# An ordered section that begins one gate group earlier, in a conv, latent-attention and memory block

## The chip, the cores and the metric

The kernel runs on one core of one Trainium2 chip. The metric is the time of one execution in device microseconds; lower is better. "Before" is the kernel as it stood, "after" is the same kernel with the diff below. Engines are named as in the profile: PE (matmuls), PEld (its weight loads), DVE, ACT, POOL and SP. SP issues the loads of weights, ACT issues most stores, POOL issues most other loads.

## The reference

512 tokens of width 2048 in float32, one layer. One input projection feeds three branches and their gates; the gated branches go through one output projection and are added to the input.

```python
h = rms_norm(x, norm_g)
(c_gate, b_gate, u, conv_z, c_q, c_kv, k_rope_raw, mla_z,
 mem_q, mem_z, g_conv, g_mla, g_mem) = split(h @ w_in)
conv_y = b_gate * causal_depthwise_conv(c_gate * u, conv_w)            # width 1024
o_conv = (conv_y * silu(conv_z)) @ w_conv_out
mla_y  = mla_attention(c_q, c_kv, k_rope_raw, cos, sin, ...)           # 16 heads
o_mla  = (mla_y * silu(mla_z)) @ w_mla_out
mem_y  = memory_attention(mem_q, mem, mem_norm_g, w_mem_kv, ...)       # 4 heads of 256
o_mem  = (mem_y * silu(mem_z)) @ w_mem_out
merged = sigmoid(g_conv) * o_conv + sigmoid(g_mla) * o_mla + sigmoid(g_mem) * o_mem
return x + merged @ w_o
```

The part around the change is the memory attention: 256 memory tokens of width 2048 are normalised and multiplied by `w_mem_kv` into keys and values; each of the four heads normalises its queries and keys, takes a softmax over the 256 tokens and multiplies by the values. The rotary tables `cos` and `sin`, which the latent attention needs later, are made in the same stretch.

## The kernel before, in words

**Products.** Every float32 operand is split into two float32r parts, a high part (`whi` for weights, rounded by ACT) and a low part (`wlo`, the rest, subtracted by DVE), and a product is three matmuls, high by high, high by low, low by high. The large projections use a two-by-two scheme with seven products, P1 to P7, in place of eight; some of them first need sums or differences of two weight blocks on DVE (`raw<-raw`). The forms of weights rotate through six buffers, which is three pairs.

**Steps.** The work is a list of steps. Each step makes the forms of one piece of weights and has 12 matmuls of 512 columns (in the stages looked at here). The forms of a step are issued one step ahead of its products. Hooks hang other work behind a step: `after(i, f)` calls `f` once step `i` is issued. `here` holds the step being issued. A gate group (`gate_group`) is 28 steps; its results are evicted from PSUM, go through a sigmoid and are stored to DRAM (`gdram<-r`). `last_s` is the first step of the last gate group, `first_m` the first step of the memory stage, 28 steps later.

**The last gate group and mem.** In the gate group hang `mem_load(j)`, four loads of the transposed memory tokens issued by POOL into `mraw`; `mem_cut(j)`, which splits each load into high and low parts `mT` (ACT and DVE, with the norm's gain) and squares it; and `mem_sum`, which adds the squares and turns them into the norm's factors with 16 matmuls of one column. The `mT` tiles lie in the buffers (tag `blk`) that hold the activations used by products P1 and P5 of the gate group.

**The memory stage.** Four weight groups of eight steps (keys, values, keys, values) with the heads hung between them. A head (`mem_attend`) is a generator in five parts, called step by step: it loads its queries (`rows<-mqdram`, two buffers, POOL), normalises, transposes and splits them (`q`), multiplies by the keys, takes the softmax (`p`), turns it (`ph`), and multiplies by the values. `rotary_tables` is hung at step 3 of the stage: loads of `pos_i`, `invf`, `rgain` and `mask` on POOL, then a chain of small operations on DVE that begins with the copy of `pos_i` to `pos_f`. `open_two`, at the stage's beginning, closes the pool `work` (tag `q` and others, which hold the gate groups' results) and opens the pools `lat`, `kv`, `memq` and `latrow` where it lay.

**Order.** Three ways stand side by side. SP's loads keep the order in which they are written. Ordinary code is put in order by the language's own scheduler. A noted section is put in order by the kernel itself: `nc.start()` begins to note every call as an `Op` (engine, estimated cost, tiles, what it depends on), and `nc.play()` runs a list scheduler over them (`order`) and issues them in that order on each engine. In it every engine is free at time zero, and an operation whose inputs were made before the section is ready at time zero. A tile that is written for the first time in the section takes a buffer of its tag; buffers of tiles that are only read in it count as taken until their last noted use; tiles that are not touched in it are not known. Among operations that could start at the same earliest time the one of lowest rank goes first. A matmul's rank is its place in the program. Other operations take the rank of the first matmul that depends on them, or their own place plus `away`:

```python
op.prio = min([op.idx + away + op.away] + [s.idx if s.eng == "PE" else s.prio for s in op.succs])
```

There are two noted sections. The first covers the beginning of the kernel. The second begins with the memory stage's third step (`TURN = 2`) and reaches to the end of the latent attention. Calls issued by a noted section bear line 250 in the profile, all other calls line 246. `nc.fence()` is called in the second section when the pools of the memory stage are closed: what first writes a tile of the pools `mla` and `proj` must then wait, in the order, for every noted operation on `latrow`, `memq` and `kv`. In the issued program every operation waits for what it really depends on, whatever the order.

Of the kernel before, what the change touches and what calls it, by code (L numbers as in the profile page):

```python
# [43 lines left out]

WARM = 5
RELAX = 600
START = 32
TURN = 2
LINE = 512
SMALL_FILL = 64  # L50
TOP_FILL = 120
# [48 lines left out]
class Player:  # L100
# [6 lines left out]
            setattr(self, n, Queue(self, getattr(nc, n), self.QUEUES[n]))  # L107

    def start(self):
        self.ops, self.access, self.first, self.fenced, self.lastpe = [], {}, {}, None, {}  # L110

    def fence(self):

        self.fenced = [o for o in self.ops
                       if any(p in str(self.first[t][1]) for t in o.tiles for p in ("_latrow_", "_memq_", "_kv_"))]

    def add(self, eng, call, kind, writes, reads):
        op = Op()
        op.eng, op.call, op.idx, op.kind, op.away = eng, call, len(self.ops), kind, self.away
        op.occ, op.lat = cost(eng, kind, writes, reads)  # L120
        op.preds, op.succs, op.gets, op.tiles = set(), [], [], []
        for ap, store in [(a, False) for a in reads] + [(a, True) for a in writes]:
            t = ap.tensor
            dims = list(ap.ap)
            on_chip = ap.space != bass.MemoryType.DRAM
            lo = ap.offset % dims[0][0] if on_chip else ap.offset
            hi = lo + sum(s * (n - 1) for s, n in dims[on_chip:]) + 1
            for o, l, h, st in self.access.setdefault(t.name, []):
                if (store or st) and l < hi and lo < h and o is not op:
                    op.preds.add(o)  # L130
            self.access[t.name].append((op, lo, hi, store))
            if on_chip:
                if t.name not in self.first:
                    self.first[t.name] = (op, str(t.cap_key), t.tag_meta.bufs)
                    op.gets.append(t.name)
                    if any(p in str(t.cap_key) for p in ("_mla_", "_proj_")):
                        op.preds.update(self.fenced)
                elif self.first[t.name][0] is not op:
                    op.preds.add(self.first[t.name][0])
                if t.name not in op.tiles:  # L140
                    op.tiles.append(t.name)
                if store and eng == "PE":
                    if t.name in self.lastpe:
                        op.preds.add(self.lastpe[t.name])
                    self.lastpe[t.name] = op
        for o in op.preds:
            o.succs.append(op)
        self.ops.append(op)
# [108 lines left out]
def cost(eng, kind, writes, reads):  # L257

    n = max(int(np.prod(a.shape[1:])) for a in (writes[:1] if kind != "tensor_reduce" else reads))
    if kind == "dma_start":  # L260
        return {"SP": (max(0.45, n * LOAD), 4.5), "ACT": (0.37, 4.5), "POOL": (0.7, 5.0)}[eng]
    if eng == "PE":
        occ = 0.109 if kind == "transpose" else max(n, 136) / 2250
        return occ, occ + 0.25
    if eng == "ACT":
        occ = 0.0009 * n + (0.045 if reads[0].space != bass.MemoryType.PSUM else 0.02)
        occ += 0.09 * (len(reads) > 1) + 0.1 * (len(writes) > 1)
    elif eng == "DVE":
        occ = n / 960 + 0.067 + 0.06 * (kind == "scalar_tensor_tensor")
    else:  # L270
        occ = 0.33 + 0.165 * n
    return occ * ROOM, occ * ROOM + 0.2


def body(ctx, tc, a, out):
    nc = Player(tc.nc)
# [4 lines left out]
    def open_pool(name, side="left", bufs=1):  # L281
        es = ExitStack()
        p = es.enter_context(tc.tile_pool(name=name, bufs=bufs, side=side, reuse_waits="tile"))
        return Lines(p, small, name), es.close
# [14 lines left out]
    def split(src, hi, lo, g=None):  # L299
        act.activation(hi, src, AF.Copy, scale=1.0 if g is None else g)  # L300
        if g is None:
            vec.tensor_tensor(out=lo, in0=src, in1=r32(hi), op=ALU.subtract)
        else:
            vec.scalar_tensor_tensor(out=lo, in0=src, scalar=g, in1=r32(hi),
                                     op0=ALU.mult, op1=ALU.subtract)

    def mm3(o, s, m, start, stop, shared=False):


        nc.tensor.matmul(o, lhsT=s[0], rhs=m[0], start=start, stop=False, skip_group_check=shared)  # L310
        nc.tensor.matmul(o, lhsT=s[0], rhs=m[1], start=False, stop=False, skip_group_check=shared)
        nc.tensor.matmul(o, lhsT=s[1], rhs=m[0], start=False, stop=stop, skip_group_check=shared)
# [31 lines left out]
    def g(col):  # L344
        return gains[:, col:col + 1]
# [30 lines left out]
    def q(name, dtype=F32):  # L376
        return work.tile([P, 2, 512], dtype, tag="q", name=name, bufs=NQ)
# [4 lines left out]
    def blk(name="blk", dtype=F32R):  # L382
        return ph.tile([P, 2, 512], dtype, tag="blk", name=name, bufs=8)
# [9 lines left out]
    def flat(t):  # L393
        return t.rearrange("p k n -> p (k n)")
# [49 lines left out]
    here = [0]  # L444

    def run_range(i0, i1):
        ws = steps[i0].forms()
        for i in range(i0, i1):
            here[0] = i
            for p in steps[i].parts:  # L450
                p(ws)
                yield
            if i + 1 < i1:
                ws = steps[i + 1].forms()
            for f in steps[i].after:
                f()

    def run_all(gen):
        for _ in gen:
            pass  # L460
# [145 lines left out]
    def after(i, f, front=False):  # L606
        steps[i].after.insert(0 if front else len(steps[i].after), f)
# [224 lines left out]
    def t_results(put, direct, early=None, add=None, own=True):  # L832
# [4 lines left out]
        def results(name, bk):  # L837
# [9 lines left out]
            if name == "P5":  # L847
                for tt in range(2):
                    vec.tensor_tensor(out=v[:, tt], in0=bk["Z"][tt], in1=v[:, tt], op=ALU.add)
                if add:  # L850
                    vec.tensor_tensor(out=flat(v), in0=flat(v), in1=flat(add(1, 1)), op=ALU.add)
                if early:
                    early(0, 1)
# [8 lines left out]
            if name in ("P4", "P6") and seen >= {"P4", "P6"}:  # L862
                r = q("r")
                for tt in range(2):
                    vec.tensor_tensor(out=r[:, tt], in0=bk["Y"][tt], in1=u[:, tt], op=ALU.add)
                if add:
                    vec.tensor_tensor(out=flat(r), in0=flat(r), in1=flat(add(0, 1)), op=ALU.add)
                    vec.tensor_tensor(out=flat(u), in0=flat(u), in1=flat(add(1, 0)), op=ALU.add)
                put(0, 1, r)
                if early:  # L870
                    early(0, 0)
# [88 lines left out]
    last_s = len(steps)  # L960
# [5 lines left out]
    def mem_load(j):  # L966
        mraw[j] = q("mraw")
        nc.gpsimd.dma_start(flat(mraw[j]).rearrange("p (k m) -> p k m", k=4), a["memT"][:, 4 * j:4 * j + 4])

    def mem_cut(j):  # L970
        m = flat(mraw[j]).rearrange("p (k m) -> p k m", k=4)
        for c in range(2):
            t = blk("mT")
            for k in range(2):
                n = 4 * j + 2 * c + k
                cols = slice(k * M, (k + 1) * M)
                split(m[:, 2 * c + k], t[:, 0, cols], t[:, 1, cols], g(G_MEM + n))
                mT[n] = (t[:, 0, cols], t[:, 1, cols])
        act.activation(flat(mraw[j]), flat(mraw[j]), AF.Square)
# [13 lines left out]
        vec.tensor_scalar(out=me, in0=v, scalar1=EPS, scalar2=None, op0=ALU.mult)  # L993

    for j in range(4):
        after(last_s + 15 + j, lambda j=j: mem_load(j))
        after(last_s + 20 + j, lambda j=j: mem_cut(j))

    P2 = {}

    def open_two():
        close_work()
        for name in ("lat", "kv", "memq", "latrow"):
            P2[name], P2["close_" + name] = open_pool(name, "left")

    first_m = len(steps)
# [39 lines left out]
    for grp in (0, 2, 1, 3):  # L1046
        d_group(a["w_mem_kv"][grp], mT, "acc", mem_results(grp), "T", nb=2)
    end_m = len(steps)
    after(first_m - 1, mem_sum)
    after(first_m - 1, open_two)  # L1050


# [69 lines left out]
    lat = {}  # L1122

    def rotary_tables():
        nc.away = RELAX
        rotary_work()
        nc.away = 0

    def rotary_work():
        pc, pcr = P2["lat"], P2["latrow"]  # L1130
# [127 lines left out]
    for s, f in ((3, rotary_tables), (20, latent_loads), (22, key_scales), (23, key_rotary), (26, query_scale)):  # L1258
        after(first_m + s, f)
# [3 lines left out]
    early_steps = run_range(0, end_m)  # L1263
    for i in range(first + 16 + START):
        next(early_steps)
        if i == first + 15:
            mark = len(nc.ops)
    nc.play(tc, (), len(nc.ops) - mark, 100)
    while here[0] < first_m + TURN:
        next(early_steps)  # L1270
    nc.start()
    run_all(early_steps)

    cqT, ckT = [None] * 4, [None] * 4
# [28 lines left out]
    key_blocks()  # L1303
    for name in ("latrow", "memq", "kv"):
        P2["close_" + name]()
    nc.fence()
    pa, close_a = open_pool("mla", "left")
    pp, close_p = open_pool("proj", "left")
    cosq, sinq = lat["tabs"]["q"]
# [436 lines left out]
```

## Time and profile before

| | |
|---|---|
| three runs, median (lowest to highest) | 2101.43 us (2100.23 to 2102.2) |
| profiled execution, its own time | 2101.0 us |
| its span, first to last instruction | 2099.1 us |
| mean granted clock of PE | 0.998 |
| busy: PE, PEld, DVE, ACT, POOL | 99%, 85%, 78%, 50%, 7% of the span |
| last gate group on PE | about 1119 to 1200 us |
| memory stage's weight products on PE | 1200 to 1321 us |

Busy time is the time in which an engine has an instruction under way. In a row of the order of time stand start, length, engine, line, operation, output and inputs, and in brackets the idle time of the engine before it and what it waited for. In the windows view each row is one stretch: its length, then for each engine busy time and instructions, the granted clock, the share of the DMA engines and GB/s.

### The profile page before, as it was taken

The numbers are of one execution on the slowest core, as the hardware profiler recorded it, in microseconds if no ns is written. First come the engines' busy times: TensorE is split into PE (matmuls) and PEld (weight loads), VectorE is DVE, ScalarE is ACT, GpSimd is POOL, SyncE is SP. The second block draws the span as 40 slices with busy tenths as digits, with TensorE's granted clock in tenths as the row PEclk, the third lists the DMA queues.
The fourth block names the chain that finished last, engine by engine and source line by source line (L and its number), as shares of the span: only waits on it lengthen the run. The fifth ranks groups of instructions, "written<-read, shape, count | busy, mean of one in ns | idle before, by whom it ended". The sixth has DMA issues, their size and how long they took to land.

```text
span 2099.1 us, 28548 instructions
## 1 busy us (share of the span) xinstructions
PE 2080.2 (99%) x10818; PEld 1792.6 (85%) x10818; DVE 1640.9 (78%) x2162; ACT 1059.5 (50%) x1524; POOL 148.4 (7%) x183
## 2 busy tenths in 40 slices
PE   9999999999999999999999989999999999999999
PEld 9888888887899988899888878888988888888887
DVE  6887788788777787777787777888887688867987
ACT  6544344344444445444445556577776344433543
POOL 0000000000000000000000011123221201110000
PEclk9999999999999999999999999999999999999999
DMA  7346444444534445534546554422332767675672
GB/s 262 124 161 201 134 137 143 144 135 133 189 121 124 148 131 184 177 121 149 167 144 225 201 187 156 146 71 78 109 106 96 289 227 203 207 230 176 202 241 75
DMA packets 106331, 338.66 MB, mean 161 GB/s; under 512 B 11088, under 2 KB 11616, under 8 KB 106192
## 3 DMA queue, kind: packets, MB, share of 16 engines
q1 hardware_dynamic: 71360, 251.92, 36.9%
q0 software_dynamic: 13792, 45.57, 7.2%
q10 hardware_dynamic: 21040, 39.33, 5.0%
q8 instruction: 85, 1.39, 0.3%
q14 instruction: 54, 0.44, 0.1%
HBM read 292.61 MB, written 44.17 MB: 160 GB/s over the span
## 4 chain that ended last, share of the span: by engine, by line
PE 95%; DVE 2%; issue 1%; DMA 1%; ACT 1%; POOL 0%; ACTq 0%; DVEq 0%; POOLq 0%
PE aux L246 38%; PE acc L246 30%; PE aux L250 14%; PE acc L250 14%; DMA raw<-in_w_ckv 0%; DVE wlo L246 0%; DVE cv L246 0%; DVE raw L246 0%; ACT whi L246 0%; DVE wlo L250 0%; DMA raw<-in_w_mlaz 0%; DMA pos_i<-in_pos 0%; DVE ang L250 0%; DVE r L246 0%; DVE s L246 0%
## 5 line engine op out<-in xcount | busy, mean ns | idle before, releaser
L246 ACT ACTIVATE whi<-raw 128x1024 fp32r<-128x1024 f32 x491 | 519.2, 1060 | 745.5 <-PE aux L246 342.6
L246 DVE TENSOR_TENSOR wlo<-raw,whi 128x1024 fp32r<-128x1024 f32 x491 | 596.8, 1221 | 276.9 <-ACT whi L246 274.1
L246 DVE TENSOR_TENSOR raw<-raw 128x1024 f32<-128x1024 f32 x258 | 315.0, 1222 | 9.2 <-DMA raw<-in_w_mla_out 1.9
L246 PE MATMUL aux<-whi,b 128*128 128x512 f32 x896 | 293.2, 389 | 1.4 <-ACT whi L246 1.4
L246 PE MATMUL aux<-whi,f 128*128 128x512 f32 x880 | 289.7, 390 | 0.0
L246 PE MATMUL acc<-whi,b 128*128 128x512 f32 x880 | 287.2, 390 | 0.8 <-ACT whi L246 0.7
L246 PEld LDWEIGHTS aux<-whi,b 128*128 128x128 f32 x896 | 168.0, 188 | 37.0 <-ACT whi L246 2.2
L246 PEld LDWEIGHTS acc<-whi,b 128*128 128x128 f32 x880 | 164.8, 188 | 35.6 <-ACT whi L246 1.9
L246 PEld LDWEIGHTS aux<-whi,f 128*128 128x128 f32 x880 | 165.0, 188 | 34.3 <-ACT E L246 0.3
L246 PE MATMUL aux<-wlo,b 128*128 128x512 f32 x448 | 174.4, 389 | 0.0
L246 PE MATMUL aux<-wlo,f 128*128 128x512 f32 x440 | 172.1, 391 | 1.0 <-DVE wlo L246 0.9
L246 PE MATMUL acc<-wlo,b 128*128 128x512 f32 x440 | 171.7, 390 | 0.0
L250 DVE TENSOR_TENSOR wlo<-raw,whi 128x1024 fp32r<-128x1024 f32 (+3 forms) x122 | 135.4, 1116 | 38.9 <-ACT whi L250 30.5
L250 ACT ACTIVATE whi<-raw 128x1024 fp32r<-128x1024 f32 (+3 forms) x122 | 118.1, 975 | 93.1 <-PE acc L250 48.6
L246 PE MATMUL acc<-whi,f 128*128 128x512 f32 x448 | 140.5, 389 | 0.0
L246 PEld LDWEIGHTS aux<-wlo,f 128*128 128x128 f32 x440 | 82.6, 188 | 20.1 <-DVE wlo L246 3.0
L246 PEld LDWEIGHTS aux<-wlo,b 128*128 128x128 f32 x448 | 84.1, 188 | 17.7 <-DVE wlo L246 0.2
L246 PEld LDWEIGHTS acc<-whi,f 128*128 128x128 f32 x448 | 84.1, 188 | 17.5
L246 PEld LDWEIGHTS acc<-wlo,b 128*128 128x128 f32 x440 | 82.6, 188 | 17.0
L246 PE MATMUL acc<-wlo,f 128*128 128x512 f32 x224 | 87.2, 389 | 0.0
L250 POOL TENSOR_TENSOR rs_r<-rs_t,mhalf 128x2 f32<-128x2 f32 (+1 forms) x71 | 69.9, 987 | 217.8 <-DVE rs_t L250 182.0
L246 POOL DMA_DIRECT2D mraw<-in_memT x4 | 2.3, 582 | 1082.7 <-DMA gdram<-r 1070.2
(392 smaller groups left out, 4096.9 us busy)
## 6 DMA issues: line engine op xcount, KB each, us to landing
raw<-in_w_conv SPq DMA_DIRECT2D x80, 512.0 KB, 4.0
raw<-in_w_gmem SPq DMA_DIRECT2D x44, 512.0 KB, 4.0
raw<-in_w_mla_out SPq DMA_DIRECT2D x44, 512.0 KB, 4.9
raw<-in_w_o SPq DMA_DIRECT2D x44, 512.0 KB, 4.4
raw<-in_w_gconv SPq DMA_DIRECT2D x40, 512.0 KB, 4.3
raw<-in_w_gmla SPq DMA_DIRECT2D x40, 512.0 KB, 3.8
raw<-in_w_mlaz SPq DMA_DIRECT2D x32, 512.0 KB, 4.2
raw<-in_w_mem_kv SPq DMA_DIRECT2D x32, 512.0 KB, 3.9
```

Of the source, the lines that this page charges most:

```text
L246: return f(*args, **kw)
L250: self.player.add(self.eng, lambda: f(*args, **kw), kind, writes, reads)
```

## The change

`TURN` goes from 2 to -24: the second noted section begins 24 steps before the memory stage, behind the products of step 4 of the last gate group. What is noted there up to the memory stage's first step gets `AWAY = 300` added to its place (`AWAYTO = 0`), so that work on which no matmul depends ranks later. The loads of mem hang at steps 8 to 11 of the gate group instead of 15 to 18, the cuts at steps 12, 15, 18 and 21 instead of 20 to 23, the sum at step 24 instead of 27. `fence` now takes the pools that it is about and keeps a list; a second call in `open_two` lets whatever first writes a tile of `lat`, `kv`, `memq` or `latrow` wait, in the order, for every noted operation on `work`. `rotary_tables` puts back the value of `away` that it found.

```diff
+AWAY, AWAYTO = 300, 0
 START = 32
-TURN = 2
+TURN = -24
...
-        self.ops, self.access, self.first, self.fenced, self.lastpe = [], {}, {}, None, {}
-
-    def fence(self):
-
-        self.fenced = [o for o in self.ops
-                       if any(p in str(self.first[t][1]) for t in o.tiles for p in ("_latrow_", "_memq_", "_kv_"))]
+        self.ops, self.access, self.first, self.fences, self.lastpe = [], {}, {}, [], {}
+
+    def fence(self, closed, opened):
+
+        if self.ops is not None:
+            self.fences.append(([o for o in self.ops if any(p in str(self.first[t][1]) for t in o.tiles
+                                                            for p in closed)], opened))
...
-                    if any(p in str(t.cap_key) for p in ("_mla_", "_proj_")):
-                        op.preds.update(self.fenced)
+                    for old, opened in self.fences:
+                        if any(p in str(t.cap_key) for p in opened):
+                            op.preds.update(old)
...
     for j in range(4):
-        after(last_s + 15 + j, lambda j=j: mem_load(j))
-        after(last_s + 20 + j, lambda j=j: mem_cut(j))
+        after(last_s + 8 + j, lambda j=j: mem_load(j))
+        after(last_s + 12 + 3 * j, lambda j=j: mem_cut(j))
...
     def open_two():
         close_work()
+        nc.fence(("_work_",), ("_lat_", "_kv_", "_memq_", "_latrow_"))
...
-    after(first_m - 1, mem_sum)
+    after(last_s + 24, mem_sum)
     after(first_m - 1, open_two)
...
     def rotary_tables():
-        nc.away = RELAX
+        usual, nc.away = nc.away, RELAX
         rotary_work()
-        nc.away = 0
+        nc.away = usual
...
     while here[0] < first_m + TURN:
         next(early_steps)
     nc.start()
+    nc.away = AWAY
+    while here[0] < first_m + AWAYTO:
+        next(early_steps)
+    nc.away = 0
     run_all(early_steps)
...
-    nc.fence()
+    nc.fence(("_latrow_", "_memq_", "_kv_"), ("_mla_", "_proj_"))
```

## The prediction

> **What bounds the kernel.** I read the page first, for the engine shares and the slices of the span, then the list of PE's waits, the chain that ended last where the longest wait is, and the order of time of the engines there.
>
> ```profile
> span 2099.1 us, 28548 instructions
> PE 2080.2 (99%) x10818; PEld 1792.6 (85%) x10818; DVE 1640.9 (78%) x2162; ACT 1059.5 (50%) x1524; POOL 148.4 (7%) x183
> PE   9999999999999999999999989999999999999999
> ```
>
> PE works nearly without a break, so a change of order alone can win only PE's idle time, 2099.1 - 2080.2 = 18.9 us, and what the clock loses around it. One slice is below nine tenths, at about 1210 to 1260 us: the beginning of the memory stage. By stages, in the windows view (PE, PEld, DVE, ACT and POOL busy, then granted clock and DMA):
>
> ```profile
> 1119.00:1200.00 81.00, 80.53 (x363) 66.51 (x363) 69.62 (x76) 48.02 (x60) 3.29 (x5) 1.00 0.57 185
> 1200.00:1262.00 62.00, 54.83 (x276) 45.56 (x275) 41.66 (x82) 36.33 (x81) 10.13 (x14) 0.94 0.59 196
> 1262.00:1640.00 378.00, 377.46 (x2116) 335.51 (x2115) 299.96 (x794) 258.11 (x603) 92.06 (x107) 1.00 0.34 111
> ```
>
> The last gate group runs in the first row, the memory stage in the second and in the beginning of the third, attention after it. The noted section now begins about 1207. Its later part leaves 0.54 us idle in 378; the stretch at its front leaves 7.17 in 62. The waits of PE between 1207 and 1262 (in all, times, longest):
>
> ```profile
> PE acc L250 <- DVE wlo L250: 6.3, 1, 6.3
> PE aux L250 <- DVE p L250: 0.7, 1, 0.7
> PE aux L250 <- DVE kn L250: 0.2, 1, 0.2
> ```
>
> One wait makes nearly all of it. The chain that ended last goes through it like this:
>
> ```profile
> 1219.89 0.70 ACT q L246
> 1220.59 0.23 issue
> 1220.82 0.80 POOL rows L250
> 1221.62 0.55 POOL kraw L250
> 1222.17 3.03 DMA pos_i<-in_pos
> 1225.20 0.02 issue
> 1225.22 0.17 DVE pos_f L250
> ```
>
> A weight's low part (wlo) stands in DVE's queue behind pos_f, the first operation of the rotary tables; pos_f waits for a small load; that load stands in POOL's queue behind a load of rows, and that one waited 8.58 us for head 0:
>
> ```profile
> 1188.22 0.80 POOL L246 DMA_DIRECT2D rows<-mqdram  x1
> 1189.83 0.76 POOL L250 DMA_DIRECT2D rows<-mqdram  x1 [0.81 <-DMA gdram<-r]
> 1220.82 0.80 POOL L250 DMA_DIRECT2D rows<-mqdram  x1 [8.58 <-ACT q L246]
> 1207.39 0.17 DVE L250 MEMSET zero<- 128x128 f32 x1 [4.70 <-DMA gdram<-r]
> 1220.61 1.41 DVE L246 SCALAR_TENSOR_TENSOR q<-aux,gains,q 128x512 fp32r<-128x512 f32 x2 [5.88 <-ACT q L246]
> 1225.22 0.17 DVE L250 CAST pos_f<-pos_i 128x4 f32<-128x4 int32 x1 [3.20 <-DMA pos_i<-in_pos]
> ```
>
> L246 marks what was issued outside the noted section, L250 what was noted and put in order. All three long DVE waits (4.70, 5.88 and 3.20, together 13.8 us) come of the seam between the two. Head 0's load and its q are L246. The order does not know that head 0 holds one of the two rows buffers, so it took the third load (head 2's) for free and set it ahead of the rotary loads. It does not know either that the new pools lie where stores of the gate group are still read, so it set the memset of zero first.
>
> **What that seam costs**, from PE's own order of time:
>
> ```profile
> 1217.66 0.39 PE L250 MATMUL acc<-wlo,mT 128*128 128x512 f32 x1
> ...
> 1218.34 0.39 PE L250 MATMUL acc<-wlo,mT 128*128 128x512 f32 x1
> ...
> 1220.05 0.71 PE L250 MATMUL acc<-whi,mT 128*128 128x512 f32 x2
> 1227.03 0.80 PE L250 MATMUL acc<-wlo,mT 128*128 128x512 f32 x1 [6.28 <-DVE wlo L250]
> ...
> 1230.16 0.62 PE L250 MATMUL acc<-whi,mT 128*128 128x512 f32 x2
> ```
>
> Three matmuls start in 0.68 us, so 0.227 each. The two of 1220.05 are due to end at 1220.50, the next starts at 1227.03: 6.53 us lost. Seven start between 1227.03 and 1230.16 (3.13 us where 1.59 is the pace): the clock comes back late, 1.54 us more. Together 8.07 us. On that second term the Trainium skill bears, "TensorE: Matmul & The Clock Gate", Part 1: after an idle window of about 3.4 us PE runs at half clock until it has been busy for about as long, and the length varies from run to run. An estimate from that page is 3.4 x 0.5 = 1.7 us, which would make the sum 8.2; the trace's 1.54 agrees, and the measured value stays in the sum. By the same page a wait much shorter than the window costs only itself.
>
> **The change, part by part.**
>
> *Beginning the noting 24 steps before the memory stage (TURN).* Nothing is added on the chip; no instruction, byte or semaphore's work is different in count. Head 0's load, its squares, its transposes and q, and all four rows tiles come inside the section. The order then knows that the third rows load needs head 0's transposes, and the rotary loads no longer have to stand behind it. This takes away the chain above: -8.07 us. What is late next is found below under the rivals. The seam itself moves to step 4 of the gate group. The first memory product stands at 1200.4:
>
> ```profile
> L246 PE MATMUL acc<-whi,mT x20: 389/389/389, 1200.4 to 1207.0; 128*128 128x512 f32 x20
> ```
>
> A step is 12 matmuls, 2.72 us at the pace above; 24 steps before 1200.4 is 1135 for PE, and the forms are made a step or two ahead of it, so the seam lies near 1131. What can stand wrongly at a seam is what the order takes for ready at its own time zero: loads into buffers still in use, and first writes of new pools. There it finds only the four loads of mem (POOL, nothing else in its queue) and weight forms that come in their natural order. I price the new seam at 0; its cover is the lead of the forms over PE (six form buffers, three steps). Its bounds: below, nothing; above, the old seam again, 8.07.
>
> *Loading, splitting and summing mem at earlier steps.* The words speak of smaller pieces; the diff leaves the bodies of the three functions alone. It is the same four loads, sixteen splits, four squares and three adds, hung at other steps, the splits three steps apart instead of one.
>
> ```profile
> 1107.23 0.73 POOL L246 DMA_DIRECT2D mraw<-in_memT  x1 [1061.14 <-DMA gdram<-r]
> ...
> 1130.59 0.53 POOL L246 DMA_DIRECT2D mraw<-in_memT  x1 [9.05 <-DMA gdram<-r]
> L246 ACT ACTIVATE mT<-mraw,gains x16: 492/493/496, 1147.0 to 1164.5; 128x256 fp32r<-128x256 f32 x16
> L246 DVE SCALAR_TENSOR_TENSOR mT<-mraw,gains,mT x16: 476/478/479, 1148.4 to 1167.4; 128x256 fp32r<-128x256 f32 x16
> L246 DVE TENSOR_TENSOR mraw<-mraw x3: 1216/1218/1224, 1156.6 to 1172.3; 128x1024 f32<-128x1024 f32 x3
> DMA to landing us min/median/max: 3.9/5.3/6.2
> ```
>
> The loads already issue by 1130.59 and land by about 1136, and between their old and new steps no other buffer of that tag is taken, so they keep their buffers and times. The splits write where the gate group's P1 and P5 operands lie; they begin at 1147.0 because product P5 has to be done with them, and no hook can make that sooner. DVE's part is 16 x 0.478 + 3 x 1.22 = 11.3 us, and it had 81.00 - 69.62 = 11.4 us idle in the gate group's stretch. Price 0, under that idle time. With the cover gone, where they stand ahead of forms, up to 11.3 us; below, the one small wait of PE there:
>
> ```profile
> PE aux L246 <- ACT whi L246: 0.5, 1, 0.5
> ```
>
> *The lower rank for the gate group's other work (AWAY).* Evictions, sigmoids and stores of the group rank 300 places later. They only fill gaps, but they free accumulators that the memory stage takes. Forms outrank them, and the forms run out of buffers after three steps, so gaps come. Price 0, covered by DVE's 11.4 us idle; uncovered, the last group's eviction adds of about 0.7 us each stand before the first memory product, a few us.
>
> *The fence.* First writes of the lat, kv, memq and latrow pools are put after every noted operation on the work pool, the last store of the group included. That ends the 4.70 us wait of zero at DVE's head. It also forbids the early rows loads of 1188.22 and 1189.83: they come after the store is down, 1207.4. That is 19 us later on POOL's queue, with the rotary loads behind them. PE has dense products of the memory stage to run meanwhile, eight steps of 2.72 for the first weight group, up to about 1222. Price 0 under those; bounds in the first rival. The kept value of away around the tables changes nothing, since it is 0 there.
>
> **The sum.** The profiled execution took 2101.0 us, 1.9 more than its span, and the runs shown have a median of 2101.43, so it stands 0.4 below. From 2101.0: -8.07 for the seam. The small waits of the stretch, 0.5 + 0.7 + 0.2 = 1.4 us, partly go and partly come anew because everything up to the end of the attention is laid out again; the row of 0.54 us idle in 378 says that such an order leaves little. I put them at 2.0 instead of 1.4, +0.6. That gives 2093.5 us. If they all go, 2101.0 - 8.07 - 1.4 = 2091.5; with another microsecond or two of new ones, 2095.
>
> **The rivals.**
>
> *The wait comes back behind the fence.* Head 0's squares began at 1207.01, just as the fence opens:
>
> ```profile
> 1201.95 0.37 ACTq L246 DMA_DIRECT2D gdram<-r  x1
> 1207.01 0.40 ACT L246 ACTIVATE sq<-rows 128x256 f32<-128x256 f32 x1
> DMA to landing us min/median/max: 3.8/6.8/9.2
> ```
>
> A rows load issued at 1207.4 lands 6.8 us later, 1214.2, so head 0's chain is 7.2 us later than now. If q then stands at the head of ACT's and DVE's queues as it does now, the forms behind it are late by up to 7.2, and 1.54 of clock follows: 8.7 against the 8.07 won, 2101.6, the same. For it: q did block DVE for 5.88 us. Against: this time the order knows when the load lands and can set forms ahead; nothing needs head 0's q before its scores, which also need the first weight group's keys, evicted and turned after 1222. Half of it would be 2097.
>
> *Slower: the splits of mem stand too early in the order.* Each of the four cuts waits for a P5 product to let go of its operands. If the order sets a cut two steps of 2.72 us (12 matmuls of 0.227) too early, ACT and DVE hold all forms behind it for 5.4 us, four times: 21.8 us, 2101.0 - 8.07 + 21.8 = 2114.7. It decides from 12.3 us, 3.1 us per cut; one step each (10.9 us, 2103.8) is still within what can be told apart. For it: DVE is full where these splits run:
>
> ```profile
> 1160.00:1180.00 20.00, 19.53 (x86) 15.80 (x86) 20.00 (x26) 10.53 (x14) 0.00 (x0) 1.00 0.27 87
> ```
>
> Against: the order's own cost of such a matmul, 512/2250 = 0.2276 us, is within 0.5% of the 0.227 measured, so it knows the release of each operand to well under a step, and the three steps between the cuts leave room.
>
> *The stall is hidden anyway.* It would have to be made up later for the change to be worth nothing. PE is busy 377.46 of the next 378 us, so nothing makes it up; I leave it no chance of its own.
>
> **How the numbers follow.** About 0.2% (4.2 us) is what a measurement of this kernel can tell from no change. The seam's wait goes and only small ones come: 0.65, 2091 to 2097, taken at 2093.5. The wait comes back in part or whole: 0.22, 2096 to 2103, of which a third is still faster by over 0.2%. The splits or the late evictions stand in the way: 0.13, 2100 to 2115 and more, mostly slower. That makes faster 0.72, same 0.17, slower 0.11. From 2091 to 2102 some 0.86 is held; the likeliest case's own range is 2091 to 2097.
>
> **What would show it.** In the changed profile: L250 operations from about 1131; no PE wait over 2 us from 1119 to 1262; granted clock 1.00 in that stretch; the slice of eight tenths back at nine; the third rows load after the rotary loads on POOL; zero no longer waiting for a gate store; head 0's rows load after 1200. Wrong if PE waits for wlo behind q or mT, or for an accumulator at the first memory product.

## The result, and the profile after

| | before | after |
|---|---|---|
| median of the runs timed side by side (lowest to highest) | 2101.81 us (2100.23 to 2103.39) | 2090.58 us (2090.26 to 2091.75) |
| ratio, 95% interval | | 0.9947 [0.9934, 0.996] |
| profiled execution, its span | 2101.0 us, 2099.1 us | 2090.99 us, 2089.2 us |

The kernel became faster by 11.2 us by medians and by 10.0 us from profiled execution to profiled execution. Forecast were 2093.5 us and a range of 2091.0 to 2102.0: the direction is right, the gain was larger than forecast, and the time lies 0.4 us below the range. In the changed kernel noted calls bear line 253 and all others line 249. Its page, first the span and the busy times, then the slices:

```profile
span 2089.2 us, 28542 instructions
PE 2077.5 (99%) x10818; PEld 1792.6 (86%) x10818; DVE 1642.0 (79%) x2162; ACT 1060.1 (51%) x1525; POOL 149.8 (7%) x183
PE   9999999999999999999999999999999999999999
```

The slice of eight tenths is gone. The two stretches of the gate group and of the stage's beginning in the windows view (length, then PE, PEld, DVE, ACT and POOL busy, granted clock, DMA share, GB/s):

```profile
1119.00:1200.00 81.00, 81.00 (x366) 67.06 (x365) 69.45 (x78) 46.59 (x59) 0.00 (x0) 1.00 0.50 157
1200.00:1262.00 62.00, 61.95 (x317) 52.08 (x316) 47.86 (x90) 41.97 (x92) 15.69 (x20) 1.00 0.69 238
```

In the second row PE is busy 61.95 us instead of 54.83 and does 317 matmuls instead of 276; the granted clock is 1.00 instead of 0.94. From 1119 to 1640 us the list of PE's waits has one line left:

```profile
PE acc L253 <- DVE qt L253: 0.5, 1, 0.5
```

The engines around the old seam, in order of time (start, length, engine, line, operation, tiles, idle before and what ended it):

```profile
1129.81 3.50 DVE L253 TENSOR_TENSOR raw<-raw 128x1024 f32<-128x1024 f32 x3
...
1200.89 1.55 POOL L253 DMA_DIRECT2D rows<-mqdram  x2
...
1204.39 0.54 POOL L253 DMA_DIRECT2D pos_i<-in_pos  x1
...
1222.56 0.80 POOL L253 DMA_DIRECT2D rows<-mqdram  x1 [4.69 <-DVE rs_t L253]
...
1210.31 0.17 DVE L253 MEMSET zero<- 128x128 f32 x1
...
1221.13 0.16 DVE L253 CAST pos_f<-pos_i 128x4 f32<-128x4 int32 x1
...
1223.10 1.40 DVE L253 SCALAR_TENSOR_TENSOR q<-aux,gains,q 128x512 fp32r<-128x512 f32 x2
```

The third rows load now stands behind the rotary loads, `pos_i` is asked for at 1204.39 instead of 1222.17, and `zero`, `pos_f` and `q` have no idle time in brackets: each stands in DVE's queue at a place where its input is there. The 1129.81 row is the first noted one on DVE; noted loads of mem issue on POOL from 1053.46 on.

**Where the 10 us came from.** Two groups of PE bracket the noted section's reach in both kernels: the products `aux<-b,whi`, all done well before the last gate group, and the part of `acc<-whi,acth` that is not noted, which begins after the noted section. A row gives their count, least, median and longest length in ns, and first and last start. Before, then after:

```profile
L246 PE MATMUL aux<-b,whi x384: 283/283/283, 614.6 to 968.9; 128*128 128x256 f32 x192
L246 PE MATMUL acc<-whi,acth x96: 389/389/477, 1651.2 to 1915.5; 128*128 128x512 f32 x96
```

```profile
L249 PE MATMUL aux<-b,whi x384: 282/283/284, 614.7 to 969.0; 128*128 128x256 f32 x192
L249 PE MATMUL acc<-whi,acth x96: 388/389/477, 1640.8 to 1905.9; 128*128 128x512 f32 x96
```

From the last start of the one to the first start of the other there are 682.3 us before and 671.8 after, 10.5 less; 0.1 was lost ahead of that stretch and 0.5 behind it. This length, called the stretch below, is compared in the experiments too, as it leaves out what happens elsewhere; run 1 has none, since its profiled execution was a slow one (2958.88 us at a granted clock of 0.656). Where in the stretch, PE's order of time tells, taken from start to start. Before:

```profile
1170.26 0.84 PE L246 MATMUL acc<-whi,f 128*128 128x512 f32 x3
1171.58 0.74 PE L246 MATMUL aux<-whi,b 128*128 128x512 f32 x2 [0.47 <-ACT whi L246]
1172.16 0.40 PE L246 MATMUL acc<-wlo,f 128*128 128x512 f32 x1
1172.39 0.63 PE L246 MATMUL acc<-whi,f 128*128 128x512 f32 x2
...
1234.94 0.39 PE L250 MATMUL acc<-whi,mT 128*128 128x512 f32 x1
1235.52 0.33 PE L250 MATMUL aux<-ident,kn 128*128 128x128 f32 x1 [0.19 <-DVE kn L250]
...
1247.64 0.39 PE L250 MATMUL acc<-whi,mT 128*128 128x512 f32 x1
1248.73 0.63 PE L250 MATMUL aux<-ident,p 128*128 128x128 f32 x4 [0.70 <-DVE p L250]
...
1376.77 1.43 PE L250 MATMUL aux<-ident,s 128*128 128x128 f32 x6
1378.57 0.50 PE L250 MATMUL acc<-whi,ckT 128*128 128x512 f32 x1 [0.37 <-DVE qt L250]
```

And after, the two places where something is left:

```profile
1237.93 0.61 PE L253 MATMUL acc<-whi,mT 128*128 128x512 f32 x2
1238.60 0.63 PE L253 MATMUL aux<-ident,p 128*128 128x128 f32 x4
1238.98 0.48 PE L253 MATMUL acc<-wlo,mT 128*128 128x512 f32 x1
...
1367.04 0.82 PE L253 MATMUL aux<-ident,s 128*128 128x128 f32 x6
1368.33 0.50 PE L253 MATMUL acc<-whi,ckT 128*128 128x512 f32 x1 [0.47 <-DVE qt L253]
```

The pace is 0.227 us for a matmul of 512 columns and 0.095 for one of 128 (four in 0.38 from 1238.60). Start to start less pace:

| place | before | after |
|---|---|---|
| gate group, `whi` (1171.58 - 1170.26 - 0.68; then three in 0.81) | 0.64 + 0.13 | 0 |
| seam, `wlo` (the prediction's 6.53 and 1.54) | 8.07 | 0 |
| `kn` | 0.35 | 0 |
| `p` | 0.86 | 0.22 |
| attention, `s` and `qt` (six of 128 columns in 1.80, in 1.29) | 1.23 | 0.72 |
| sum | 11.28 | 0.94 |

The difference is 10.3 of the 10.5 us. The seam is the 8.07 us that the prediction took; the small waits gave 2.3 us on top. In the attention the wait for `qt` itself did not shrink (0.37 shown before, 0.47 after). What went lies in the row ahead of it, six transposes of `s` in 1.43 us before and 0.82 after: before, their weight loads waited 0.41 and 0.30 us for ACT to finish `s`.

### The profile page after: what moved, and what is told of

It reads as the page before. It is cut to its first block, busy times and chain, and to the rows that moved or that the text cites. A ratio compares the mean times of both kernels' runs of the same rounds, so it can differ in the third digit from the quotient of the medians.

```text
span 2089.2 us, 28542 instructions
## 1 busy us (share of the span) xinstructions
PE 2077.5 (99%) x10818; PEld 1792.6 (86%) x10818; DVE 1642.0 (79%) x2162; ACT 1060.1 (51%) x1525; POOL 149.8 (7%) x183
## 4 chain that ended last, share of the span: by engine, by line
PE 96%; DVE 2%; DMA 1%; issue 1%; ACT 0%; POOL 0%; SPq 0%; DVEq 0%; ACTq 0%; POOLq 0%
PE aux L249 36%; PE acc L249 28%; PE acc L253 16%; PE aux L253 16%; DVE wlo L249 0%; DMA raw<-in_w_mla_out 0%; DVE cv L249 0%; DVE raw L249 0%; DMA xraw<-in_xT 0%; ACT whi L249 0%; DVE r L249 0%; DMA gains<-in_gains 0%; DVE s L249 0%; POOL rs_r L253 0%; ACT cv L249 0%
## 5 line engine op out<-in xcount | busy, mean ns | idle before, releaser
L249 ACT ACTIVATE whi<-raw 128x1024 fp32r<-128x1024 f32 x465 | 491.6, 1060 | 717.3 <-PE aux L249 329.1
L249 DVE TENSOR_TENSOR wlo<-raw,whi 128x1024 fp32r<-128x1024 f32 x465 | 566.0, 1223 | 268.8 <-ACT whi L249 263.9
L249 DVE TENSOR_TENSOR raw<-raw 128x1024 f32<-128x1024 f32 x244 | 298.3, 1224 | 9.9 <-DMA raw<-in_w_mla_out 3.1
L249 PE MATMUL acc<-whi,b 128*128 128x512 f32 x840 | 274.1, 390 | 0.8 <-ACT whi L249 0.7
L249 PE MATMUL aux<-whi,f 128*128 128x512 f32 x832 | 273.9, 390 | 0.0
L249 PE MATMUL aux<-whi,b 128*128 128x512 f32 x832 | 272.4, 390 | 1.0 <-ACT whi L249 1.0
L253 DVE TENSOR_TENSOR wlo<-raw,whi 128x1024 fp32r<-128x1024 f32 (+3 forms) x148 | 167.1, 1136 | 52.3 <-ACT whi L253 41.1
L253 ACT ACTIVATE whi<-raw 128x1024 fp32r<-128x1024 f32 (+3 forms) x148 | 145.3, 990 | 122.2 <-PE acc L253 58.5
L253 POOL TENSOR_TENSOR rs_r<-rs_t,mhalf 128x4 f32<-128x4 f32 (+1 forms) x72 | 71.0, 989 | 216.8 <-DVE rs_t L253 172.2
L253 PE MATMUL acc<-whi,mT 128*128 128x512 f32 x256 | 81.5, 393 | 0.0
```

The costliest lines, as they stand in the source:

```text
L249: return f(*args, **kw)
L253: self.player.add(self.eng, lambda: f(*args, **kw), kind, writes, reads)
```

## The experiments

**Theories.** The seam theory: the seam at the front of the noted section is nearly the whole of it. Head 0 is issued outside, so the order places loads and operations that it believes free, and they block POOL and then DVE; whatever brings head 0 inside takes the 8 us away, and the other parts of the change are worth little. The hooks theory: the hooks of mem (loads, cuts, sum) give DVE room and are the gain. The length theory: the length of the noted section is the gain, so that a longer one brings more. The medians stand against runs of the kernel before on the same chip.

| kernel | median | before there | ratio, 95% | stretch |
|---|---|---|---|---|
| before | | | | 682.3 |
| changed kernel | 2090.58 | 2101.81 | 0.9947 [0.9934, 0.996] | 671.8 |
| 1 hooks alone | 2101.61 | 2101.03 | 1.0 [0.999, 1.0009] | |
| 2 section from the stage on | 2092.51 | 2101.03 | 0.9953 [0.9938, 0.9968] | 674.0 |
| 3 changed, old hooks | 2092.06 | 2101.03 | 0.9951 [0.9936, 0.9966] | 673.8 |
| 4 one hook of head 0 | 2092.07 | 2101.03 | 0.9951 [0.9934, 0.9967] | 673.4 |
| 5 changed, old sum | 2092.4 | 2101.69 | 0.9954 [0.9936, 0.9972] | 674.0 |
| 6 changed, old loads and cuts | 2090.48 | 2101.69 | 0.9945 [0.9929, 0.996] | 671.8 |
| 7 TURN = -12 | 2089.72 | 2101.69 | 0.994 [0.9924, 0.9956] | 671.2 |
| 8 changed, no lower rank | 2091.46 | 2101.69 | 0.9949 [0.9934, 0.9965] | 673.0 |
| 9 before, tables hung later | 2101.1 | 2100.97 | 1.0 [0.9991, 1.001] | 682.7 |
| 10 TURN = -370 | 2106.57 | 2100.97 | 1.0025 [1.0016, 1.0034] | 672.2 |
| 11 TURN = -12 again | 2089.27 | 2100.97 | 0.9942 [0.9929, 0.9956] | 671.2 |
| 12 changed kernel again | 2090.68 | 2100.97 | 0.995 [0.9937, 0.9962] | 671.7 |
| 13 before, tables loaded by SP | 2092.84 | 2101.2 | 0.9957 [0.994, 0.9973] | 673.7 |

### 1. The hooks alone

```diff
 # on the kernel before
-        after(last_s + 15 + j, lambda j=j: mem_load(j))
-        after(last_s + 20 + j, lambda j=j: mem_cut(j))
+        after(last_s + 8 + j, lambda j=j: mem_load(j))
+        after(last_s + 12 + 3 * j, lambda j=j: mem_cut(j))
...
-    after(first_m - 1, mem_sum)
+    after(last_s + 24, mem_sum)
```

> The kernel before with only the hooks of mem moved (loads at steps 8 to 11, cuts at 12, 15, 18, 21, sum at 24); the section still begins at the memory stage's third step. Seam theory (the loss is head 0's load, transposes and q being issued outside the noted section): nothing changes at 1220, PE still waits about 6.3 us for a low part, time 2101 to 2102.5. Mem theory (mem's splits crowd DVE in the gate group, and moving them is part of the gain): the 0.5 us wait near 1171 goes and the forms enter the memory stage with more lead, 1.5 to 3 us faster, 2098.5 to 2100.

Measured: 2101.61 us, ratio 1.0 [0.999, 1.0009]. PE's wait for `wlo` is still in the trace, with 6.1 us. Without the longer section the hooks bring nothing. The hooks theory falls as the cause of the gain.

### 2. The section from the memory stage on

```diff
 # on the changed kernel; loads, cuts and sum at their old steps
-TURN = -24
+TURN = -1
```

> The kernel after with the section beginning at the last step of the gate group (TURN = -1) and mem's hooks where they were: the whole memory stage is noted, the gate group is not. Seam theory: head 0 is inside, so the 6.53 us wait, the slow restart of 1.54 and the waits of 0.7 and 0.2 behind it are gone; the 0.5 us wait near 1171 in the gate group stays: 9.4 us faster than before on the profile, time 2091.3 to 2093. Rival (the seam needs distance from the memory stage): with the seam only one step ahead, the first writes of the new pools stand at the head of DVE or POOL for the stores of the gate group, some 5 us as in the kernel before, and PE waits 2 to 6 us again: 2095 to 2099.

Measured: 2092.51 us. PE's waits from 1119 to 1340:

```profile
PE acc L253 <- DVE wlo L253: 0.5, 1, 0.5
PE aux L253 <- DVE p L253: 0.5, 1, 0.5
PE aux L249 <- ACT whi L249: 0.5, 1, 0.5
```

The wait of 6.3 us is gone with only three steps more in the section, which are enough to have all of head 0 in it. Small waits of the old kind stay, the gate group's among them. That is the seam theory for the 8 us, and it shows that the rest of the gain, about 2 us, hangs on something else.

### 3. The changed kernel with the old hooks

```diff
 # on the changed kernel
-        after(last_s + 8 + j, lambda j=j: mem_load(j))
-        after(last_s + 12 + 3 * j, lambda j=j: mem_cut(j))
+        after(last_s + 15 + j, lambda j=j: mem_load(j))
+        after(last_s + 20 + j, lambda j=j: mem_cut(j))
...
-    after(last_s + 24, mem_sum)
+    after(first_m - 1, mem_sum)
```

> The kernel after (section from 24 steps before the stage, with rank and fence) but mem's hooks at their old steps. Seam theory: the hooks are worth nothing, because a noted section sets mem's work by readiness and rank: within 0.6 us of the changed kernel, 2090 to 2091.5, and no PE wait over 0.5 us from 1119 to 1262. Mem theory: at least 1.5 us slower than the changed kernel, 2092 or more, with PE waits in the gate group or at the first memory products.

Measured: 2092.06 us. The waits in the gate group and at `p` are gone, but a new one stands in the list:

```profile
PE aux L253 <- ACT mkh L253: 1.4, 1, 1.4
```

So inside the longer section the hooks do matter, by some 1.5 us, against the seam theory's forecast of 0.6 at most; nor is the wait where the other theory looked for it. Which of the hooks matter, runs 5 and 6 tell.

### 4. One number: head 0's second part inside the section

```diff
 # on the kernel before
-    for s, h in ((0, 0), (1, 0), (2, 1), (8, 0), ...
+    for s, h in ((0, 0), (2, 0), (2, 1), (8, 0), ...
```

> The kernel before with one number changed: the second part of head 0 (squares, norm, transposes, q) hangs at step 2 of the memory stage instead of step 1, so it is noted, and the order sees that head 0 holds a rows buffer. Seam theory: the third rows load no longer stands ahead of the rotary loads, q is set among the forms, and most of the 8.07 us goes: 2093 to 2096, the rest being the memset of zero that still waits 4.7 us at DVE's head. Rival (it takes the fence and the whole stage): PE still waits 3 us or more for a low part, 2097.5 to 2101.

Measured: 2092.07 us, 9.0 us below the kernel before on that chip and 0.9 below the seam theory's range. `TURN` is 2 as before, there is no fence on `work`, and the load of head 0 is still issued outside; only its squares, transposes and q are noted. The order of time of POOL and DVE:

```profile
1204.59 0.54 POOL L250 DMA_DIRECT2D pos_i<-in_pos  x1
...
1216.45 0.77 POOL L250 DMA_DIRECT2D rows<-mqdram  x1 [3.69 <-ACT q L250]
...
1208.63 0.17 DVE L250 MEMSET zero<- 128x128 f32 x1 [4.17 <-DMA gdram<-r]
```

The third rows load now stands behind the rotary loads. `zero` still waits 4.17 us for the gate group's store, and no PE wait comes of it: of the three DVE waits that the prediction put down to the seam, that one costs nothing here. In the changed kernel, with the fence, it is gone; for these 9.0 us the fence is not needed.

### 5. The changed kernel with the old hook of the sum

```diff
 # on the changed kernel
-    after(last_s + 24, mem_sum)
+    after(first_m - 1, mem_sum)
```

> The changed kernel with the sum of mem's squares hung at the last step of the gate group again; loads and cuts stay moved. With all three hooks put back PE waited 1.4 us for the keys' high parts (mkh), because ACT stood 2.1 us for a late rows load. Theory that the early sum matters (its 16 matmuls stood at 1190 instead of 1198): that wait is back, 1.5 us slower than the changed kernel, 2091.8 to 2092.5. Rival (each layout has its own small waits, and no hook stands for any): another wait of 0 to 1.5 us at another place, or none, 2090.3 to 2092.

Measured: 2092.4 us, 1.8 above the changed kernel; the stretch is 2.2 longer. ACT and PE in order of time:

```profile
1231.23 0.42 ACT L253 ACTIVATE sq<-rows 128x256 f32<-128x256 f32 x1 [2.39 <-DMA rows<-mqdram]
...
1232.15 0.50 PE L253 MATMUL aux<-mkh,q 128*128 128x256 f32 x2 [1.68 <-ACT mkh L253]
```

The squares of the third rows tile stand ahead of `mkh`, the keys that PE needs at once, and wait 2.39 us for their load. In the changed kernel the order is the other way round:

```profile
1228.32 1.57 ACT L253 ACTIVATE mkh<-aux,gains 128x256 fp32r<-128x256 f32 x4 [0.17 <-PE aux L253]
```

It is the old fault in small: an operation whose load is late at the head of an engine's queue. That the sum's hook brings it is shown; by which step of the order it does, is not.

### 6. The changed kernel with the old hooks of loads and cuts

```diff
 # on the changed kernel; the sum stays at last_s + 24
-        after(last_s + 8 + j, lambda j=j: mem_load(j))
-        after(last_s + 12 + 3 * j, lambda j=j: mem_cut(j))
+        after(last_s + 15 + j, lambda j=j: mem_load(j))
+        after(last_s + 20 + j, lambda j=j: mem_cut(j))
```

> The changed kernel with loads and cuts of mem at their old steps and the sum left at step 24. Theory that the early sum matters: no wait of PE over 0.5 us from 1119 to 1340, 2090.3 to 2091.2. Theory that the cuts matter: the mkh wait of 1.4 us is back, 2092. Rival (layout): anything from 2090.3 to 2092.5 with waits at other places.

Measured: 2090.48 us, stretch 671.8, no PE wait from 1119 to 1340. Loading and splitting mem sooner is worth nothing; of the three hooks the sum's alone counts, and only inside the section (run 1).

### 7 and 11, 12. A section that begins 12 steps before the stage

```diff
 # on the changed kernel
-TURN = -24
+TURN = -12
```

> The changed kernel with the section beginning 12 steps before the memory stage instead of 24, so that the loads and the first cuts of mem are issued outside it. Seam theory: head 0 is inside, so nothing of the 8.07 us comes back; what differs is small waits only, 2090.5 to 2092.5. Rival (where the seam stands among mem's splits matters): DVE is full there and the order does not know of the outstanding splits, PE waits 2 us or more near 1170, 2093 to 2096.

> The seam 12 steps ahead again, beside the changed kernel on the same chip, to see whether it beats both. Theory (one small wait fewer, 0.22, and 0.4 of slower matmuls less than the changed kernel): 0.5 to 1 us faster than the changed kernel. Rival (the difference seen between sessions was the start of the run): within 0.3 us of it.

> The changed kernel itself, unaltered, for comparison on one chip with the two kernels with other seams: 2090.3 to 2091.5, no PE wait over 0.5 us from 1119 to 1340.

Measured: 2089.72 us, and in five rounds beside the unaltered changed kernel 2089.27 (2089.04 to 2089.52) against 2090.68 (2089.97 to 2092.51). It beats both kernels: the ratio to the kernel before is 0.9942 [0.9929, 0.9956]. Run 11, then run 12:

```profile
L249 PE MATMUL aux<-b,whi x384: 282/283/284, 614.0 to 968.4; 128*128 128x256 f32 x192
L249 PE MATMUL acc<-whi,acth x96: 388/389/477, 1639.6 to 1904.0; 128*128 128x512 f32 x96
```

```profile
L249 PE MATMUL aux<-b,whi x384: 282/283/284, 615.0 to 969.4; 128*128 128x256 f32 x192
L249 PE MATMUL acc<-whi,acth x96: 389/389/477, 1641.1 to 1905.3; 128*128 128x512 f32 x96
```

Of the 1.5 us between the last lines, 1.0 is there already at 969 us, ahead of anything that `TURN` orders differently; in the rows of the table with a stretch that point lies between 968.4 and 970.8 us, the tenth apart. In the stretch the shorter section is worth 0.5 us (671.2 in both of its profiles, 671.7 and 671.8 in those of the changed kernel); what makes the rest of the 1.4 us between the medians is not shown. Run 7 lies below both of its forecasts. The length theory is not borne out.

### 8. The changed kernel without the lower rank

```diff
 # on the changed kernel
-AWAY, AWAYTO = 300, 0
+AWAY, AWAYTO = 0, 0
```

> The changed kernel with AWAY = 0: evictions and stores of the gate group rank by their place. Theory that the rank costs and wins nothing: 2090.3 to 2091.5, no PE wait over 0.5 us. Theory that it pays for the small waits: evictions stand before forms while DVE is full, PE waits 0.5 to 2 us between 1119 and 1207, 2091.5 to 2093.

Measured: 2091.46 us, 0.8 to 0.9 above the changed kernel's medians, the stretch 1.2 longer. The gate group has no wait, where the second theory looked for one. But PE's wait for `p` is back in the list (0.7 us), and in the attention the six transposes of `s` ahead of `qt` again take 1.75 us from start to start instead of 1.29. The rank is worth about 1 us, at places far from the work that it ranks.

### 9. The kernel before with the tables hung nine steps later

```diff
 # on the kernel before
-    for s, f in ((3, rotary_tables), (20, latent_loads), ...
+    for s, f in ((12, rotary_tables), (20, latent_loads), ...
```

> The kernel before with one number changed: the rotary tables hang at step 12 of the memory stage instead of step 3; head 0's q is issued outside the section as before. It tells the two halves of the seam's wait apart, q at the head of DVE (5.88 us, done at 1222.0) and pos_f behind it (3.20 us more). Theory of both in series: with pos_f gone the low part runs right after q, at about 1222, PE goes on at 1223.3 instead of 1227.0, and with the shorter gap the slow restart shrinks: 3.7 to 5 us faster, 2096.5 to 2098. Rival (q does it all): PE still waits 6 us, 2101. Rival (pos_f and the loads in POOL's queue do it all): the whole 8.07 us goes, 2093.

Measured: 2101.1 us, ratio 1.0 [0.9991, 1.001]. This was to part the share of `pos_f` from that of q, and did not, since nothing moved:

```profile
1221.02 1.41 DVE L246 SCALAR_TENSOR_TENSOR q<-aux,gains,q 128x512 fp32r<-128x512 f32 x2 [5.87 <-ACT q L246]
...
1220.45 0.71 PE L250 MATMUL acc<-whi,mT 128*128 128x512 f32 x2
1227.50 0.79 PE L250 MATMUL acc<-wlo,mT 128*128 128x512 f32 x1 [6.34 <-DVE wlo L250]
...
1232.65 0.40 PE L250 MATMUL acc<-wlo,mT 128*128 128x512 f32 x1
```

The loads of the rotary tables and `pos_f` have no inputs from the section, so the order takes them for ready at its start, and here nine steps in the program did not move them. The three PE rows are used below.

### 10. A section that begins 370 steps before the stage

```diff
 # on the changed kernel
-TURN = -24
+TURN = -370
```

> The changed kernel with the section beginning 370 steps before the memory stage, ahead of the convolution's groups, where PE still has 3.4 us of small waits between 200 and 1119 in the profile of the changed kernel. Theory that a noted section leaves fewer small waits anywhere: 1.5 to 3 us faster than the changed kernel, 2087.5 to 2089. Rival (the order's cost model drifts from the chip over 1000 us, or the low rank of evictions holds accumulators): new waits of 2 to 10 us in the groups, 2092 to 2100.

Measured: 2106.57 us, ratio 1.0025 [1.0016, 1.0034], slower than before. The stretch is as good as in the changed kernel (672.2); the loss lies ahead of it, where the last `aux<-b,whi` starts at 985.3 instead of 969.0. PE's wait for `cv` from 200 to 1117 us (in all, times, longest), and DVE and PE at the longest:

```profile
PE aux L253 <- DVE cv L253: 12.9, 4, 5.7
```

```profile
360.64 1.22 DVE L253 TENSOR_TENSOR raw<-raw 128x1024 f32<-128x1024 f32 x1
361.78 1.53 DVE L253 SCALAR_TENSOR_TENSOR cv<-cu,gains,cv 128x512 f32<-128x512 f32 x2
363.35 0.69 DVE L253 TENSOR_TENSOR cv<-aux,cv 128x512 f32<-128x512 f32 x1
...
364.19 1.09 PE L253 MATMUL aux<-ident,r 128*128 128x128 f32 x4 [5.71 <-DVE cv L253]
```

The convolution's `cv`, whose last operation frees an accumulator (`aux`) for PE, was put behind weight forms. The length theory falls: over this work the same order is worse than the one it replaces. Whether the rank or the estimated costs put `cv` there was not tried.

### 13. The kernel before with the rotary loads on SP

```diff
 # on the kernel before; likewise for invf, rgain and mask
-        nc.gpsimd.dma_start(pos_i, a["pos"])
+        nc.sync.dma_start(pos_i, a["pos"])
```

> The kernel before with one thing changed: the four small loads of the rotary tables are issued by SP instead of POOL, so that they no longer stand behind the third rows load; head 0's q still stands at DVE's head. Theory of two halves in series: pos_f's wait of 3.2 us is gone, the low part runs right after q at about 1222, PE stands for 2.8 instead of 6.5 us and restarts less slowly: 3.7 to 5 us faster than before, 2096.5 to 2098. Rival (q does it all): PE still waits 6 us, 2101. Rival (the loads behind the rows load do it all, and without them DVE's forms go ahead of q): 8 us faster, 2093. Rival (slower): SP stands for the pools' buffers until 1207 and holds weight loads: a wait for raw takes the place, 2100 or more.

Measured: 2092.84 us, 8.4 below the kernel before on that chip. POOL and DVE in order of time:

```profile
1222.58 0.80 POOL L250 DMA_DIRECT2D rows<-mqdram  x1 [8.63 <-PE acc L250]
...
1222.37 1.23 DVE L250 TENSOR_TENSOR wlo<-raw,whi 128x1024 fp32r<-128x1024 f32 x1 [1.56 <-PE acc L250]
1223.51 1.40 DVE L246 SCALAR_TENSOR_TENSOR q<-aux,gains,q 128x512 fp32r<-128x512 f32 x2
...
1225.61 0.16 DVE L250 CAST pos_f<-pos_i 128x4 f32<-128x4 int32 x1
```

The third rows load still stands blocked for 8.63 us, and head 0 is still outside. Yet PE's wait of 6.3 us is gone; 0.7 for `p` and 0.5 for `whi` are all that stay from 1119 to 1340. So here the blocked load by itself costs PE nothing; only what stands behind it can. Two things changed on DVE, though: `pos_f` no longer waits, and q stands behind seven low parts of the noted section instead of four, so that the one that PE lacked before now goes ahead of both. That the pile-up behind the load on POOL made the stall, as the prediction's chain has it, fits this run but is not shown by it alone: what q's 5.88 us and `pos_f`'s 3.20 us each cost stays open.

## Why the prediction was right, and where not

- **The seam, -8.07.** Right in place, and right that head 0's being outside makes it: it is gone in every kernel that brings head 0's second part into the section (2 to 8 and 10 to 12), by one number alone (4). It also goes when the rotary loads leave the blocked queue (13), but how the stall divides between q and the chain through POOL stays open. The size holds for the execution from which it was read; in run 9 the same stall cost 6.60 + 2.43 = 9.03 us, with a slower restart. The medians of 2, 4 and 13 lie 8.4 to 9.0 below those of the kernel before.
- **The small waits, +0.6: the step that failed.** They were put at 2.0 instead of 1.4. Measured they went from 3.21 (0.77 + 0.35 + 0.86 + 1.23) to 0.94, -2.3 us. With that, 2101.0 - 8.07 - 2.3 = 2090.6, beside 2090.99 in the profiled execution; this term alone takes the sum below the range. Three things were wrong in it. It was taken from the idle time that the list of waits shows, and start to start the same places cost more: `p` 0.86 for 0.70, `whi` 0.77 for 0.47, `kn` 0.35 for 0.19. It left out the attention, where the 0.54 us idle in 378 hid a loss of 1.23 at `s` and `qt`, of which 0.5 went. And new small waits were assumed to come as others go, while this layout had next to none. The range's low end was set half a microsecond under the case of all shown waits gone, and so too high.
- **The hooks of mem at 0.** Right for loads and cuts (6), wrong for the sum: inside the section it saves 1.8 us (5), the wait for `mkh` behind late squares. It is part of the same failed term; the prediction had looked for the hooks' effect on DVE's room only.
- **The lower rank at 0.** Worth about 1 us (8), at `p` and at `s` ahead of `qt`.
- **The new seam at 0.** Right: no PE wait between 1119 and 1340, and the first noted operation on DVE at 1129.81 against a forecast of about 1131. The loads of mem did not keep their times: they issue from 1053.46 to 1113.99 instead of 1107.23 to 1130.59, at no cost.
- **The fence at 0.** No PE wait speaks against the price, but no run takes the fence alone out of the changed kernel. The reason given for it was wrong: the first two rows loads came at 1200.89, not 1207.4, ahead of the group's last two stores, issued at 1202.29 and 1202.76. The fence puts them behind those stores in the order only; on the chip nothing made them wait. For the seam's gain it was not needed (4).
- **The rivals.** The wait behind the fence did not come back: q stands at 1223.10 with its input there. The splits did not hold the forms: with the cuts three steps apart or one (6) PE waits for none. The stall was not hidden: of the 10.5 us won in the stretch only 0.5 was lost again behind it.
- **Profile against median.** The profiled execution of before lies 0.8 under its median of six and that of after 0.4 above; the other 1.2 us between 10.0 and 11.2 is this.

## What to carry to other kernels

An order made for one section of a program is blind at its front: what was issued just before it still holds buffers and queues. Take whole chains into it, so that each load and the work that frees its buffer are either both inside or both outside; here one number did four fifths of the change. Look for one blocked load with unrelated loads behind it on the same queue; moving those to another queue took the stall away here too (13), though the order on DVE changed with it. Count waits from start to start, let the range include that all small ones go, and do not expect a longer ordered section to be a better one.

## What the runs showed of the hardware

The restart after a gap of about 6.5 us cost 1.54 us in the kernel before; in run 9, after a shown wait of 6.34 us, twelve matmuls from 1227.50 to 1232.65 took 5.15 us where 2.72 is the pace, 2.43 lost. (The gap itself: the two of 1220.45 are due to end at 1220.90, so 6.60.) The Trainium skill ("TensorE: Matmul & The Clock Gate", Part 1) says that the half clock lasts about 3.4 us and that its length varies; by it an estimate is 1.7 us. The traces bear out the variation, and run 9's slow stretch of some 5 us is longer than the 3.4 us of that section. After the wait of 0.47 us in the gate group only 0.13 us more was lost, which agrees with the rule of the same section of the Trainium skill that the clock falls after at least one idle window of that length.

Whether a kernel without the gap scatters less is not settled. On one chip 21 runs of the kernel before spread over 2.3 us, five of the changed kernel (run 12) over 2.5 us and five of run 11 over 0.5 us.
